# A list scheduler sets the order of gate, scan and q/k/v in a Hymba block; 22 of 32 exponent blocks skip DRAM

## The chip, the cores and the metric

The kernel runs on one core of a Trainium2 chip. The metric is the device time of one execution in microseconds. The core has a matrix engine (TensorE, PE in the profile), VectorE (DVE), ScalarE (ACT), GpSimd (POOL) and SyncE (SP), each with a queue of its own that it works through in order, and 16 DMA engines. In this kernel SyncE issues nearly all loads, ScalarE issues the stores of the stage spoken of here.

## The reference

One layer on x of 1024 tokens by 1024 features, all in float32. The layer has two mixers in parallel behind one input projection:

```
h = rmsnorm(x)
z, xbc, dt_raw, q, k, v = split(h @ w_in)          # 1024 | 1536 | 32 | 1024 | 1024 | 1024
y_ssm = ssd_mixer(z, xbc, dt_raw, ...)             # conv, bidirectional chunked scan, gate
y_na  = neighbourhood_attention(q, k, v, ...)      # q, k normalised by head, windows on a 16 x 64 grid
x = x + concat([y_ssm, y_na]) @ w_out
x = x + square(relu(rmsnorm(x) @ w_mlp_in)) @ w_mlp_out
```

The scan has 16 heads of 64 features in 2 groups, a state of 128 and chunks of 128 tokens. For each chunk, direction and head:

```
decay  = exp(where(lower, a_cum[l] - a_cum[s], -inf))       # 128 x 128 for a head
y_diag = (C B^T * decay) @ (x dt)                           # within the chunk
h      = chunk_decay * h + B^T (x dt * decay_to_end)        # state, chunk after chunk
y_off  = (C h) * exp(a_cum)                                 # carried into the chunk
y      = (y_f + y_b + d_skip x) * silu(z), then a grouped rmsnorm
```

## The kernel before

Every product of weight and activation is made as three products of halves: an operand is split into a rounded part and the rest (h and l in the names), and `mm3` multiplies high by high, high by low and low by high. The stages run one after another: the xBC projection with its convolution and the decays (0 to 172 us), then **gate, scan and q/k/v (172 to 648.5 us), the stage that is rewritten**, attention with w_out beside it (to 1034), and the two MLP products (to 1657).

The stage makes 64 pieces, each 128 tokens by 512 columns: 8 column blocks (z0 z1 q0 k0 v0 q1 k1 v1; 0 and 1 are the halves of the heads, with the scan's group of the same number) by 8 token blocks. A piece is 8 x 3 = 24 matmuls of 128x512 into one PSUM tile (`pz`, `pq`; L181 to L183 are the three of `mm3`). The weights of a column come as four tiles of 256 rows: a load `wraw` on SyncE (L150), the high half `wh` on ScalarE (L151), the low half `wl` on VectorE (L152). The rings of `wh` and `wl` hold four tiles, so a column's tiles take the place of the last one's; that of `wraw` holds three.

What follows a piece: for z a SiLU (L649) and a store. For q and k a square on ScalarE (`normed`, L330), a sum on VectorE (`sq`, L332), (mean + eps)^-0.5 on GpSimd (`rq`, L209 and L210), the scaling on VectorE (`qn`, L334), four transposes on TensorE (`ptq`, L342), the split into halves (`hl`, L194 and L195), and the store: four DMAs for q, one for k. For v the split and one store.

The scan's work lies between the pieces, written out by hand. `beside`, called behind each gate piece, makes the 14 states of the backward direction (`weighed` and its split, L416, L186, L187; `pS`, L617) and the first 20 exponent blocks. An exponent block holds four heads of a chunk, 128 x 512, for both directions: `seg_load` (L391) broadcasts the running sums of both directions to all partitions (`rb`, 512 KB), `seg_make` subtracts on GpSimd (two of L400) and selects by the mask of the lower triangle on VectorE (L406), `seg_store` (L411) puts the block into DRAM. All 32 blocks go that way, and `prepare` loads them again (`gm`, L688) and takes the exponential (L689). Behind the gate, the loop over 16 steps (2 groups by 8 chunks) takes pieces from the generator `qkv_units` between its parts: `carry` (the forward state), `inside` (C B^T, L705, and its product with the exponentials, L721), `carried` (L732, L733), `finish` (the inner product, `pd`, L758, and the gate, L675). The calls fix which piece stands between which parts; `issue_after` pins stores and some matmuls behind a piece. Within that, the framework orders each engine's queue.

Of the kernel before, what the change touches and what calls it, by code (L numbers as in the profile page):

```python
# [19 lines left out]
P = 128  # L20
# [9 lines left out]
HD = 64  # L30

# [25 lines left out]
def hymba_block(  # L57
# [35 lines left out]
    def enter_phase(ph, i, mm, extra):  # L93
        phase["ps"] = ph.enter_context(
            tc.tile_pool(name=f"ps{i}", bufs=1, space=PSUM, reuse_waits="tile")
        )
        phase["mm"] = mm
        phase["v"] = 4 - mm
        phase["w"] = [wp] * 3
        phase["r"] = [wp] * 2  # L100
        phase["n"] = 0
        if extra:
# [16 lines left out]
    q_dr = dr.tile([8, 4, HD, T], F32, name="q_dr")  # L119
# [4 lines left out]
    seg_dr = dr.tile([2, NT, P, 2, 512], F32, name="seg_dr")  # L124
    sb_dr = dr.tile([2, NT, P, 512], F32, name="sb_dr")
# [11 lines left out]
    def load_w(view, lo_eng, n=1024):  # L137
        pool = phase["w"][phase["n"] % len(phase["w"])]
        nb = phase["w"].count(pool)
        phase["n"] += 1  # L140
        rpool = phase["r"][phase["n"] % len(phase["r"])]
# [3 lines left out]
        hi = pool.tile([P, 1024], F32R, tag="wh", name="wh", bufs=nb)  # L145
        lo = pool.tile([P, 1024], F32R, tag="wl", name="wl", bufs=nb)
# [4 lines left out]
        nc.scalar.activation(hi[:, 0:n], raw[:, 0:n], AF.Copy)  # L151
        lo_eng.tensor_tensor(  # L152
            lo[:, 0:n], raw[:, 0:n], hi[:, 0:n].bitcast(F32), op=sub
        )
        return hi, lo

# [56 lines left out]
    with ExitStack() as ph:  # L213
# [98 lines left out]

        def hb(v):
            return v.unsqueeze(2).broadcast_to([P, 8, HD])

# [3 lines left out]
        def qkv_proj(off, g):  # L319
            get = load_w_nat(w_in[0], 0, KD, off + 512 * g, nc.vector)  # L320
            for b in range(NT):
                pt = ps_mm("pq")
                for k in range(KD):
                    s = (slice(None), k, slice(b * P, (b + 1) * P))
                    mark = mm3(pt, hTh[s], hTl[s], *get(k), k == 0, k == KD - 1)
                yield b, pt, rcol[:, b : b + 1], mark.ins

        def normed(pt, rt):
            qn = hp.tile([P, 512], F32, tag="qn", name="qn", bufs=2)
            act = nc.scalar.activation(qn, pt, AF.Square, scale=rt)  # L330
            ss = hp.tile([P, 8], F32, tag="sq", name="sq", bufs=2)
            nc.vector.tensor_reduce(ss, h8(qn), axis=mybir.AxisListType.X, op=add)  # L332
            r = inv_rms(hp, ss, HD, 8, "rq")
            nc.vector.scalar_tensor_tensor(h8(qn), h8(pt), rt, hb(r), op0=mul, op1=mul)  # L334
            return qn, act.ins

        def turned_split(qn, w, mark):
            tp = ps_tp("ptq")
            with tc.issue_after(mark):
                for j in range(4):  # L340
                    s = slice(j * P, (j + 1) * P)
                    nc.tensor.transpose(tp[:, s], qn[:, s], ident)  # L342
            hl = hp.tile([P, 2, 512], F32R, tag="hl", name="hl", bufs=2)
            split_from_psum(hl[:, 0], hl[:, 1], tp, w)
            return hl.bitcast(F32).rearrange("f a (p t) -> f a p t", p=4)

        def store_q(g, b, qn, mark):
            hl = turned_split(qn, pcol[:, 80:81], mark)
            s = slice(b * P, (b + 1) * P)
            for j in range(2):  # L350
                for a in range(2):
                    nc.scalar.dma_start(
                        q_dr[4 * g : 4 * g + 4, 2 * j + (a ^ j), :, s].rearrange("p d t -> d p t"),
                        hl[j * HD : (j + 1) * HD, a],
                    )

        def store_k(g, b, qn, mark):
            hl = turned_split(qn, pcol[:, 81:82], mark)
            nc.scalar.dma_start(
                k_dr[g, :, :, :, b * P : (b + 1) * P].rearrange("a p f t -> f (a p) t"),  # L360
                hl.rearrange("f a p t -> f (a p) t"),
            )

        def qkv_units():
            held = None
            for g in range(2):
                for off in (OFF_Q, OFF_K, OFF_V):
                    for b, pt, rt, mark in qkv_proj(off, g):
                        if held is not None:
                            held(mark)  # L370
                            held = None
                        if off == OFF_V:
                            hl = hp.tile([P, 8, 2, HD], F32R, tag="hl", name="hl", bufs=2)
                            split_from_psum(hl[:, :, 0], hl[:, :, 1], h8(pt), rt)
                            nc.scalar.dma_start(v_dr[b, :, 8 * g : 8 * g + 8], hl.bitcast(F32))
                            act = None
                        else:
                            qn, act = normed(pt, rt)
                            held = partial(store_q if off == OFF_Q else store_k, g, b, qn)
                        yield mark, act  # L380
# [7 lines left out]
        def seg_load(pool, bufs, g, c, q):  # L388
            rb = pool.tile([P, 2, 4, P], F32, tag="rb", name="rb", bufs=bufs)
            r0 = c * 16 + 8 * g + 4 * q  # L390
            nc.sync.dma_start(  # L391
                rb.rearrange("p d h s -> p d (h s)"),
                cum_dr[:, r0 : r0 + 4, :].rearrange("d h s -> d (h s)").partition_broadcast(P),
            )
            return rb

        def seg_make(rb, g, c, q):
            h0 = 8 * g + 4 * q
            for d in range(2):
                nc.gpsimd.tensor_tensor(  # L400
                    rb[:, d],
                    rb[:, d],
                    c1[:, d, c, h0 : h0 + 4].unsqueeze(2).broadcast_to([P, 4, P]),
                    op=sub,
                )
            nc.vector.copy_predicated(  # L406
                rb[:, 0], lmask.unsqueeze(1).broadcast_to([P, 4, P]), rb[:, 1]
            )
# [247 lines left out]
        with ExitStack() as p2:  # L656
# [140 lines left out]
            for _ in units:  # L797
                pass
# [676 lines left out]
```

## Time and profile before

| | |
|---|---|
| runs | 1654.14, 1653.69, 1646.92 us; median 1653.69 |
| profiled execution | 1659.05 us, span 1657.3 us |
| mean granted clock of TensorE | 0.982 |
| busy in the span | PE 1589.3 us (96%), DVE 1017.6 (61%), ACT 719.1 (43%), POOL 714.6 (43%) |
| stage 172 to 648.5 us | 476.5 us: PE 450.15 busy, DVE 293.28, ACT 173.80, POOL 274.82; clock 0.98, DMA 0.78 |
| DMA of the stage | 111.41 MB, 234 GB/s |

A busy PE is one on which a matmul is under way; two matmuls behind each other overlap in the record (0.39 us each, 0.227 apart). The arrow in a row names what ended an idle time. `pq`, `pz`, `ptq`, `pd`, `pS`, `py` are PSUM tiles by their use; `rb`, `gm`, `xhl`, `shl` SBUF tiles.

### The profile page before, as it was taken

Reading aid. Unit: us, or ns where it says so; the run is one execution under the profiler, and the core shown is the slowest. Engines: PE = TensorE matmul, PEld = TensorE weight load, DVE = VectorE, ACT = ScalarE, POOL = GpSimd, SP = SyncE. Lnnn points to the kernel's source line nnn. Section 1 sums busy time; section 2 is a strip of 40 time slices with the busy share of each in tenths; the row PEclk is TensorE's granted clock in tenths of the full one; section 3 lists DMA queues with packets and bytes.
Section 4 is the critical chain, followed back from the end, with each engine's and each line's share of the span. In section 5 each row is a group of like instructions: output and inputs, shape, how many; then the busy total and the mean of one; then the engine's idle time right before and its main releaser. Section 6 shows DMA issues by size and latency. Waiting matters only on the chain. (4 is left out here: it accounts for less than half of the span.)

```text
span 1657.3 us, 20925 instructions
## 1 busy us (share of the span) xinstructions
PE 1589.3 (96%) x7462; PEld 1300.0 (78%) x7462; DVE 1017.6 (61%) x1420; ACT 719.1 (43%) x1183; POOL 714.6 (43%) x520
## 2 busy tenths in 40 slices
PE   7999988998989999999998998999999989999999
PEld 6788867877867888887887776888888868888887
DVE  4777455477657773666665477434244388887863
ACT  5434322254334344566675334444444534433330
POOL 3000266467546744232353332344444555455551
PEclk9999999999999999999999998999999989999999
DMA  8113688897877669968772430453444486644332
GB/s 207 53 38 102 194 266 260 222 304 212 271 210 191 190 196 308 270 171 206 207 218 77 131 123 26 151 180 117 146 157 140 163 295 214 216 142 150 102 102 77
DMA packets 190243, 290.28 MB, mean 175 GB/s; under 512 B 15715, under 2 KB 106939, under 8 KB 190139
## 3 DMA queue, kind: packets, MB, share of 16 engines
q1 hardware_dynamic: 141547, 239.65, 47.4%
q10 hardware_dynamic: 47584, 45.62, 8.5%
q0 software_dynamic: 1008, 3.67, 0.5%
q8 instruction: 59, 0.97, 0.2%
q14 instruction: 45, 0.37, 0.1%
HBM read 197.27 MB, written 94.95 MB: 176 GB/s over the span
## 5 line engine op out<-in xcount | busy, mean ns | idle before, releaser
L187 POOL TENSOR_TENSOR wl<-wraw,wh 128x1024 fp32r<-128x1024 f32 x110 | 298.3, 2722 | 320.0 <-ACT wh L186 305.5
L186 ACT ACTIVATE wh<-wraw 128x1024 fp32r<-128x1024 f32 x110 | 115.5, 1054 | 150.1 <-PE px L804 50.7
L804 PE MATMUL px<-wh,ahl 128*128 128x512 f32 x512 | 162.4, 395 | 3.3 <-ACT ahl L186 3.3
L182 PE MATMUL pq<-wl,hTh 128*128 128x512 f32 x384 | 152.9, 399 | 6.7 <-DVE wl L152 6.7
L181 PE MATMUL pq<-wh,hTh 128*128 128x512 f32 x384 | 152.1, 401 | 7.0 <-ACT wh L151 5.3
L804 PE MATMUL px<-h,wh 128*128 128x512 f32 x496 | 156.0, 396 | 1.6 <-DVE x L1156 1.6
L183 PE MATMUL pq<-wh,hTl 128*128 128x512 f32 x384 | 152.4, 398 | 0.0
L187 DVE TENSOR_TENSOR ahl<-ar,ahl 128x1024 fp32r<-128x1024 f32 x56 | 114.7, 2055 | 23.3 <-ACT ahl L186 22.2
L186 ACT ACTIVATE ahl<-ar 128x1024 fp32r<-128x1024 f32 x56 | 58.2, 1052 | 140.0 <-PE px L804 76.4
L804 PEld LDWEIGHTS px<-wh,ahl 128*128 128x128 f32 x512 | 97.1, 190 | 25.0 <-ACT ahl L186 3.7
L804 PEld LDWEIGHTS px<-h,wh 128*128 128x128 f32 x496 | 93.2, 188 | 24.2 <-ACT h L191 1.8
L804 PE MATMUL px<-wl,ahl 128*128 128x512 f32 x256 | 100.9, 395 | 0.0
L400 POOL TENSOR_TENSOR rb<-rb,c 128x512 f32<-128x512 f32 x64 | 71.2, 1134 | 67.6 <-DMA rb<-cum_dr 57.0
L804 PE MATMUL px<-h,wl 128*128 128x512 f32 x248 | 98.1, 395 | 0.0
L182 PEld LDWEIGHTS pq<-wl,hTh 128*128 128x128 f32 x384 | 73.4, 191 | 22.9 <-DVE wl L152 8.4
L181 PEld LDWEIGHTS pq<-wh,hTh 128*128 128x128 f32 x384 | 73.2, 191 | 22.8 <-ACT wh L151 6.6
L151 ACT ACTIVATE wh<-wraw 128x1024 fp32r<-128x1024 f32 x58 | 60.6, 1057 | 66.8 <-DMA wraw<-in_w_in_dram 30.3
L191 ACT ACTIVATE pth<-ptp 128x384 fp32r<-128x384 f32 (+1 forms) x128 | 56.9, 457 | 66.0 <-PE ptp L1014 65.5
L183 PEld LDWEIGHTS pq<-wh,hTl 128*128 128x128 f32 x384 | 73.3, 191 | 15.0
L804 PE MATMUL pz<-h,wh 128*128 128x512 f32 x256 | 82.2, 402 | 0.4 <-DVE h L192 0.4
L804 PE MATMUL pz<-wh,ahl 128*128 128x512 f32 x256 | 80.5, 391 | 0.0
L181 PE MATMUL po<-wh,yh 128*128 128x512 f32 x192 | 76.5, 398 | 2.1 <-DVE x L888 1.8
(273 smaller groups left out, 4031.9 us busy)
## 6 DMA issues: line engine op xcount, KB each, us to landing
ar<-act_dr SPq DMA_DIRECT2D x56, 512.0 KB, 3.6
act_dr<-cq SPq DMA_DIRECT2D x49, 512.0 KB, 3.0
wraw<-in_w_in_dram SPq DMA_DIRECT2D x44, 512.0 KB, 4.3
rb<-cum_dr SPq DMA_DIRECT2D x32, 512.0 KB, 6.6
wraw<-in_w_mlp_in_dram SPq DMA_DIRECT2D x32, 512.0 KB, 4.7
wraw<-in_w_mlp_out_dram SPq DMA_DIRECT2D x32, 512.0 KB, 4.3
seg_dr<-rb ACTq DMA_DIRECT2D x32, 256.0 KB, 2.9
q_dr<-hl ACTq DMA_DIRECT2D x64, 128.0 KB, 3.8
```

The source lines that it names most:

```text
L151: nc.scalar.activation(hi[:, 0:n], raw[:, 0:n], AF.Copy)
L181: nc.tensor.matmul(pt, lhsT=ah, rhs=bh, start=first, stop=False)
L182: nc.tensor.matmul(pt, lhsT=ah, rhs=bl, start=False, stop=False)
L183: return nc.tensor.matmul(pt, lhsT=al, rhs=bh, start=False, stop=last)
L186: nc.scalar.activation(hl[0], src, AF.Copy)
L187: eng.tensor_tensor(hl[1], src, hl[0].bitcast(F32), op=sub)
L191: top = nc.scalar.activation(hi, src, AF.Copy)
L400: nc.gpsimd.tensor_tensor(rb[:, d], rb[:, d], c1[:, d, c, h0 : h0 + 4].unsqueeze(2).broadcast_to([P, 4, P]), op=sub,)
L804: nc.tensor.matmul(pt, lhsT=a, rhs=b, start=f, stop=l, skip_group_check=True)
```

## The change

`beside`, the loop over steps and the generator `qkv_units` are replaced by tasks: each instruction (or three or eight matmuls that belong together) is a `Task` with its engine, a length written by hand, the buffers it reads and writes, and for some a due time. `Plan.order` runs a list scheduler over them: it takes the task that can start first, in slots of 0.35 us, and among those the one due first. A task can start when its engine is free, what it depends on is over (plus a margin of 0.9 us for TensorE, 0.25 for the others) and the buffer that it takes in its ring is free; DMAs also queue for a modelled bandwidth. The kernel then emits the tasks in that order, and `in_order` ties every instruction to the one before it on its engine, so that the framework keeps the order. Besides:

- The columns come as z0 z1 q0 v0 k0 q1 v1 k1.
- 10 exponent blocks (the second four heads of steps 0 to 9) are still stored and loaded. The other 22 are made into the tile `seg` from which the step uses them. The subtraction for one direction writes `seg` or `y`, and the select (now L824) reads `rb`'s other half, so `rb` is free after the select; its ring holds 2.
- The ring of raw weights holds four tiles in place of three.
- q is laid out in DRAM like k and stored by one DMA of 512 KB a piece in place of four of 128 KB; attention loads it by four DMAs of 256 KB in place of one of 1024 KB.
- The DMAs that build the attention's bias table get due times through the stage; before they stood at its middle.

No product is added or removed on TensorE. The core of the diff:

```diff
+SCAN_TILES = (
+    ("rb", 2, 1024, F32),
+    ("seg", 4, 512, F32),
+    ("xs", 3, 512, F32),
+    ("xw", 1, 512, F32),
...
+class Plan:
+    MARGIN = {"PE": 0.9, "ACT": 0.25, "DVE": 0.25, "POOL": 0.25, "SP": 0.25}
...
+    def order(self):
+        for t in reversed(self.tasks):
+            if t.due is None:
+                t.due = 1e9
+            for u in t.after:
+                late = t.due - u.cost - self.latency(u)
+                u.due = late if u.due is None else min(u.due, late)
...
+            for t in todo:
+                at = self.ready(t, free)
+                if at is None:
+                    continue
+                key = (round(at / 0.35), t.due)
+                if best is None or key < best[0]:
+                    best = key, at, t
...
+    def ready(self, t, free):
+        e = "ACT" if t.eng == "AQ" else t.eng
+        at = free[e]
+        for u in t.after:
+            if u.end is None:
+                return None
+            far = u.eng != t.eng or u.size
+            at = max(at, u.end + (self.MARGIN[e] if far else 0.0))
+        for b in t.new:
+            if self.asked[b.tag][0] is not b:
+                return None
+            made = self.made[b.tag]
+            n = self.rings[b.tag]
+            if len(made) >= n:
+                for u in made[-n].users:
+                    if u.end is None:
+                        return None
+                    at = max(at, u.end + 0.2)
+        return at
...
-            phase["r"] += [wx]
+            phase["r"] += [wx] * 2
...
-    q_dr = dr.tile([8, 4, HD, T], F32, name="q_dr")
+    q_dr = dr.tile([2, 2, 4, P, T], F32, name="q_dr")
...
-        def seg_store(rb, g, c, q):
-            nc.scalar.dma_start(seg_dr[g, c, :, q], rb[:, 0].rearrange("p h s -> p (h s)"))
...
+        cols = [OFF_Z, OFF_Z + 512]
+        cols += [off + 512 * g for g in range(2) for off in (OFF_Q, OFF_V, OFF_K)]
...
+                task("SP", 0.45, load, writes=[raw], size=512, name="raw")
+                task("ACT", 1.06, high, reads=[raw], writes=[w], name="wh")
+                task("DVE", 1.7, partial(low, nc.vector), reads=[raw], writes=[w], name="wl")
...
+                task("POOL", 1.06, subtract, reads=[rb], writes=[rb] if d else [seg], name="sub")
+            task(
+                "DVE",
+                0.9,
+                lambda: nc.vector.copy_predicated(
+                    heads(seg.t), lmask.unsqueeze(1).broadcast_to([P, 4, P]), heads(both()[:, 1])
+                ),
+                reads=[rb],
+                writes=[seg],
+                due=due,
+                name="select",
+            )
...
+            task("PE", 0.95, within, reads=[*gm, xs], writes=[pd], due=at + 9, name="pd")
...
+        stored = [(n, 1) for n in range(10)]
...
+        for m, (c, g) in enumerate(back):
+            last[g] = back_state(c, g, last.get(g), when(6.0 + m))
+        for m, (n, q) in enumerate(stored):
+            exponents_stored(n, q, when(4.0 + 1.4 * m))
+        for n in range(16):
+            step(n, (0,) if (n, 1) in stored else (0, 1), when(20.0 + 2.4 * n))
+        tables()
...
+        for t in plan.order():
+            for buf in t.writes:
+                if buf.tag and buf.t is None and buf.tag not in ("w", "raw"):
+                    buf.t = tile_of(buf.tag)
+            with in_order():
+                t.emit()
```

What it does to the queues, at three places. The line numbers after the change are those of the new file. First VectorE, where it makes the low halves of q's first column (`wl`), of before:

```order
L187 TENSOR_TENSOR xhl<-xw,xhl 128x512
L406 COPY_PREDICATED rb<-lmask,rb 128x512
L617 TENSOR_TENSOR st<-st,pS 128x512
L406 COPY_PREDICATED rb<-lmask,rb 128x512
L187 TENSOR_TENSOR xhl<-xw,xhl 128x512
L152 TENSOR_TENSOR wl<-wraw,wh 128x1024 x3
L617 TENSOR_TENSOR st<-st,pS 128x512
L406 COPY_PREDICATED rb<-lmask,rb 128x512
L152 TENSOR_TENSOR wl<-wraw,wh 128x1024
```

and of the change:

```order
L824 COPY_PREDICATED y<-lmask,rb 128x512
L863 TENSOR_TENSOR yo<-yo,py 128x512
L846 TENSOR_TENSOR xl<-xw,xh 128x512
L712 TENSOR_TENSOR wl<-wraw,wh 128x1024 x4
L846 TENSOR_TENSOR xl<-xw,xh 128x512
L863 TENSOR_TENSOR yo<-yo,py 128x512
L824 COPY_PREDICATED seg<-lmask,rb 128x512
```

The select that stood between the third and the fourth low half now stands three instructions behind the four; one stands three ahead of them.

Second SyncE's queue, from the loads of the second gate column to those of q's first (both `wraw`), of before:

```order
L150 DMA wraw<-in_w_in_dram 128x2x512
L631 DMA xs<-xs_dr 128x512
L391 DMA rb<-cum_dr 128x2x512 x2
L631 DMA xs<-xs_dr 128x512
L391 DMA rb<-cum_dr 128x2x512 x7
L150 DMA wraw<-in_w_in_dram 128x2x512 x4
L391 DMA rb<-cum_dr 128x2x512 x3
```

and of the change:

```order
L975 DMA t_dr<-in_rel_pos_bias_dram 16x15x24 x8
L802 DMA rb<-cum_dr 128x2x512 x2
L851 DMA xs<-xs_dr 128x512 x2
L802 DMA rb<-cum_dr 128x2x512
L851 DMA xs<-xs_dr 128x512 x2
L284 DMA wraw<-in_w_in_dram 128x2x512 x3
L802 DMA rb<-cum_dr 128x2x512
L284 DMA wraw<-in_w_in_dram 128x2x512
L802 DMA rb<-cum_dr 128x2x512
```

Seven broadcasts (`rb`) stood in a run ahead of the four weight loads; now one or two stand between other loads, and three of the four weight loads come behind the third.

Third TensorE at the end of the stage, where the scores of attention (`psc`) and the turns of w_out's input (`pty`) begin, of before:

```order
L183 MATMUL pq<-wh,hTl 128x512
L985 MATMUL psc<-k,q 128x256
L988 MATMUL psc<-kl,q 128x256
L985 MATMUL psc<-k,q 128x384
L988 MATMUL psc<-kl,q 128x384
L862 MATMUL pty<-ident,yl 128x128 x8
```

and of the change:

```order
L326 MATMUL pq<-wh,hTl 128x512
L763 MATMUL ptq<-ident,qn 128x128 x4
L1213 MATMUL psc<-k,q 128x256
L1216 MATMUL psc<-kl,q 128x256
L1213 MATMUL psc<-k,q 128x384
L1216 MATMUL psc<-kl,q 128x384
L763 MATMUL ptq<-ident,qn 128x128 x8
L1085 MATMUL pty<-ident,yl 128x128 x4
```

The last column is now k, so the last product is followed by turns (`ptq`): four transposes of one piece at once, and eight of the last two behind the scores.

More of the change, by code (lines that the diff above doesn't have):

```diff
@@ L311, in hymba_block @@
         nc.sync.dma_start(dsk, d_skip.partition_broadcast(P)[:, 0, :])
-        def hb(v):
-            return v.unsqueeze(2).broadcast_to([P, 8, HD])
-        def h8(v):
-            return v.rearrange("p (e d) -> p e d", d=HD)
[L319 to L345, printed above, removed]
@@ new lines, in tile_of, with dma, when @@
+        def tile_of(tag):
+            if tag in make:
+                return make[tag]()
+            n, w, d = shape[tag]
+            return qs.tile([P, w], d, tag=tag, name=tag, bufs=n)
+        Buf, task = plan.buf, plan.task
+        def dma(eng, out, src, cost=0.45):
+            q = nc.sync if eng == "SP" else nc.scalar
+            return lambda: q.dma_start(out() if callable(out) else out, src() if callable(src) else src)
+        def when(k):
+            return 5.7 * k if k < 16 else 91.2 + 6.15 * (k - 16)
@@ new lines, in hymba_block, with w_view @@
+        cols = [OFF_Z, OFF_Z + 512]
+        cols += [off + 512 * g for g in range(2) for off in (OFF_Q, OFF_V, OFF_K)]
+        def w_view(j, k):
+            return w_in[0][256 * k : 256 * (k + 1), cols[j] : cols[j] + 512].rearrange(
+                "(a p) f -> p a f", p=P
+            )
+        first = [split_raw(r, nc.vector) for r in [load_raw(w_view(0, k)) for k in range(4)]]
+        W = {}
+        for k in range(4):
+            plan.given(Buf("raw"))
+            W[0, k] = plan.given(Buf("w"), first[k])
@@ L797, in hymba_block @@
-            for _ in units:
-                pass
+                task("SP", 0.45, partial(lambda i: nc.sync.dma_start(t2_dr[:, i], t1_dr[:, :, 15 - i : 31 - i, :].rearrange("h j r c -> h j (r c)")), i), reads=[*zero, *diag], size=250, due=260 + 6 * i, name="t2")
+        back = [(NT - 1 - m % 7, m // 7) for m in range(14)]
+        stored = [(n, 1) for n in range(10)]
+        last = {}
+        for j in range(8):
+            if j:
+                weights(j)
+            for b in range(NT):
+                piece(j, b)
@@ new lines, in hymba_block, with in_order @@
+        for m, (c, g) in enumerate(back):
[5 more added lines that the diff above has]
+        tables()
+        behind = {}
+        @contextmanager
+        def in_order():
+            traced = nc.cur_bb.bb.instructions
+            mark = traced[-1]
+            yield
+            start = next(i for i in reversed(range(len(traced))) if traced[i] is mark) + 1
+            for ins in traced[start:]:
+                if ins.engine in behind:
+                    tc.add_manual_dep(
+                        ins,
+                        behind[ins.engine].name,
+                        mybir.DependencyInfo(
+                            mybir.DependencyClass.NoSync, mybir.DependencyReason.DATA
+                        ),
+                        reason="issue_after",
+                    )
+                behind[ins.engine] = ins
```

621 lines of the change are left out of this document (356 added, 265 removed).

## The prediction

> **What bounds the kernel now.** I read the page's busy rows first, then the windows by stage, then the groups of TensorE with what ended their waits, and last the timeline and the waits of the other queues inside the stage that changes.
>
> ```profile
> PE 1589.3 (96%) x7462; PEld 1300.0 (78%) x7462; DVE 1017.6 (61%) x1420; ACT 719.1 (43%) x1183; POOL 714.6 (43%) x520
> 172.00:325.00 153.00, 143.69 (x621) 116.49 (x620) 76.81 (x78) 39.84 (x56) 85.64 (x78) 0.96 0.78 237
> 325.00:500.00 175.00, 159.56 (x775) 131.15 (x774) 120.17 (x188) 73.90 (x127) 106.53 (x101) 0.98 0.82 249
> 172.00:648.50 476.50, 450.15 (x2138) 371.05 (x2137) 293.28 (x417) 173.80 (x285) 274.82 (x261) 0.98 0.78 234
> ```
>
> A window row gives the stretch and its length, then PE, PEld, DVE, ACT and POOL (busy, instructions), the granted clock, the DMA share and GB/s. TensorE is busy 96% of the span, so no other engine bounds the whole. Only 172.0 to 648.5 us, gate, scan and q/k/v, is rewritten, so the gain can be no more than what TensorE loses there, in waits and in clock. Its groups in that stage say what that is:
>
> ```profile
> L182 PE MATMUL pq<-wl,hTh 128*128 128x512 f32 x384 | 152.9, 399 | 6.7 <-DVE wl L152 6.7
> L181 PE MATMUL pq<-wh,hTh 128*128 128x512 f32 x384 | 152.1, 401 | 7.0 <-ACT wh L151 5.3 <-DVE qn L334 1.7
> L182 PE MATMUL pz<-wl,hTh 128*128 128x512 f32 x128 | 51.2, 400 | 2.1 <-DVE wl L152 2.1
> L181 PE MATMUL pz<-wh,hTh 128*128 128x512 f32 x128 | 50.6, 399 | 2.3 <-ACT wh L151 2.3
> L342 PE MATMUL ptq<-ident,qn 128*128 128x128 f32 x128 | 19.8, 278 | 8.1 <-DVE qn L334 6.4 <-ACT gm L689 1.6
> ```
>
> Idle time is 6.7 + 7.0 + 2.1 + 2.3 + 8.1 = 26.2 us: 18.1 at the change from one weight column to the next, 8.1 at turns. The windows add the clock: 0.04 of 153 us is 6.1 and 0.02 of 175 us is 3.5, together 9.6. **The ceiling is 26.2 + 9.6 = 35.8 us.** One column change, TensorE first, then VectorE:
>
> ```profile
> 283.58 0.79 PE L182 MATMUL pq<-wl,hTh 128*128 128x512 f32 x1 [4.90 <-DVE wl L152]
> 284.18 0.63 PE L183 MATMUL pq<-wh,hTl 128*128 128x512 f32 x1
> ```
> ```profile
> 280.27 1.55 DVE L406 COPY_PREDICATED rb<-lmask,rb 128x512 f32<-128x512 int32 x1 [2.37 <-POOL rb L400]
> 281.72 0.67 DVE L187 TENSOR_TENSOR xhl<-xw,xhl 128x512 fp32r<-128x512 f32 x1
> 282.32 4.33 DVE L152 TENSOR_TENSOR wl<-wraw,wh 128x1024 fp32r<-128x1024 f32 x3
> ```
> ```profile
> ACT wh L151 <- DMA wraw<-in_w_in_dram: 29.9, 7, 10.5
> POOL rb L400 <- DMA rb<-cum_dr: 57.0, 20, 10.6
> DVE rb L406 <- POOL rb L400: 49.2, 24, 6.8
> ```
>
> The weights' low half stands in VectorE's queue behind a select that waits for a GpSimd subtraction, which waits for a broadcast transfer. TensorE idles 4.90 us, and the matmul after it takes 0.63 us instead of 0.40: half clock. The last fence totals such waits in the stage (sum, times, longest): late transfers, passed on by engines that keep their order.
>
> **The change, part by part.** *TensorE's work* is the same: 64 pieces of 24 products, the scan's products and the turns. Nothing there can give time but the 35.8 us.
>
> *Order.* The planner issues a column's four weight loads ahead of the broadcasts on SyncE, and VectorE makes all four low halves in one run (the order rows above). Each of the four links of the stall is thereby moved ahead of its use. I count the whole 35.8 us as removed, and add back what the new order brings.
>
> *Exponents.* 22 stores and 22 loads of 256 KB go, the 32 broadcasts of 512 KB stay. With 64 stores of q replaced by 16, ScalarE issues 70 transfers fewer (22 + 48). It was busy 173.80 of 476.50 us, so that lies beside TensorE: 0 us beyond the waits already counted. The bytes saved are 44 × 0.26 = 11.5 of 234 GB/s × 476.5 us = 111 MB; the DMA share stays near 0.78 × 0.9 × 476.5 / 458 = 0.73. Loads should land no later than before, and how late they were is in the 35.8: I take 0. If the saved bytes mattered for nothing but the waits on transfers, the worth is within that ceiling; if the share rose with the shorter stage, the loss is that of rival D.
>
> *Column changes that stay.* Even with raw weights in time, the four buffers of a column are reused by the next. Two rows of one change in the middle of the stage show the price where nothing was late:
>
> ```profile
> 353.06 0.96 PE L181 MATMUL pq<-wh,hTh 128*128 128x512 f32 x3 [0.41 <-ACT wh L151]
> 354.89 0.50 PE L182 MATMUL pq<-wl,hTh 128*128 128x512 f32 x1 [0.39 <-DVE wl L152]
> ```
>
> 0.41 + 0.39 = 0.8 us, seven changes: **+5.6 us**. If it were nothing 0, if all were like the late one above 7 × 4.9 = 34.
>
> *The dense stretch.* The new column order q, v, k puts k of the first half and q of the second back to back (from the start of piece 33 to that of 48, 15 pieces), and their normalising falls on VectorE together with the scan. By the order VectorE gets 8 low halves, 11 selects, 15 reductions, 15 scalings, 14 q/k low halves, 17 splits of scan operands, 13 decay products, 11 scalings of a carried part, 6 gate products and some 33 small or single ones. Their rows in the stage of before:
>
> ```profile
> L152 DVE TENSOR_TENSOR wl<-wraw,wh 128x1024 fp32r<-128x1024 f32 x29 | 38.5, 1347 | 0.8 <-ACT wh L151 0.8
> L406 DVE COPY_PREDICATED rb<-lmask,rb 128x512 f32<-128x512 int32 x32 | 39.6, 1239 | 54.2 <-POOL rb L400 49.2 <-DMA sz_dr<-zs 3.7 <-DMA wraw<-in_w_in_dram 1.3
> L332 DVE TENSOR_REDUCE sq<-qn 128x8 f32<-128x512 f32 x32 | 21.6, 677 | 4.7 <-ACT qn L330 4.6
> L334 DVE SCALAR_TENSOR_TENSOR qn<-pq,rcol,rq 128x512 f32<-128x512 f32 x32 | 24.0, 749 | 28.0 <-POOL rq L210 28.0
> L187 DVE TENSOR_TENSOR xhl<-xw,xhl 128x512 fp32r<-128x512 f32 x28 | 25.2, 900 | 21.7 <-ACT xhl L186 21.5
> 581.00:597.00 16.00, 16.00 (x86) 13.56 (x85) 14.62 (x22) 9.98 (x16) 12.29 (x11) 1.00 0.56 164
> ```
>
> Low halves, selects, reductions, scalings and splits come to 10.8 + 13.6 + 10.2 + 11.2 + 15.3 = 61.1 us, the other 77 at the mean of the second window (120.17 / 188 = 0.64) to 49: **some 110 us of VectorE**. TensorE's share of the same stretch, from three more prices:
>
> ```profile
> 1368.69 10.89 PE px L804 x48
> 303.22 0.60 PE L342 MATMUL ptq<-ident,qn 128*128 128x128 f32 x4
> 303.58 0.48 PE L181 MATMUL pq<-wh,hTh 128*128 128x512 f32 x1
> 579.27 1.90 PE L758 MATMUL pd<-xs,gm 128*128 128x64 f32 x16
> 580.97 0.48 PE L181 MATMUL pS<-xhl,bNh 128*128 128x512 f32 x1
> ```
>
> 10.89 / 48 = 0.227 a product, 0.36 a turn of four, 1.70 the inner product of a step. 15 pieces × 24 × 0.227 = 81.7, 45 scan products 10.2, 13 turns 4.7, 6 steps 10.2, some 1 for the rest: 108 us. VectorE would be the longer here. The last row of the fence before shows it filled to 14.62 of 16 us (91%) while TensorE never stopped; at that fill 110 / 0.91 = 121, a loss of 13. From below: a split can take 0.67 us (the row at 281.72) against its mean of 0.90; with 17 × 0.23, and 11 selects shorter in the same ratio (0.32 each), VectorE needs 7.4 us less, 103, which TensorE's 108 covers, and the loss is 0. I take **+7 us**, the middle: the row at 581 us speaks for the first end, the short splits for the second.
>
> The Trainium skill (page "SBUF — State Buffer", section "Who interferes with whom") says a VectorE instruction with two SBUF inputs contends with a GpSimd one that reads SBUF, and the later fully blocks. That speaks against so dense a stretch. The trace bears it out in part only: rival C below works out from rows what such an exclusion would cost here.
>
> *The end of the stage.* Before, v came last; now k of the second half does, whose last pieces must still be squared, reduced, normalised and turned. TensorE's queue holds the last two turns behind only four score products.
>
> ```profile
> 648.26 0.39 PE L183 MATMUL pq<-wh,hTl 128*128 128x512 f32 x1
> 648.49 0.28 PE L985 MATMUL psc<-k,q 128*128 128x256 f32 x1
> 649.07 1.04 PE L862 MATMUL pty<-ident,yl 128*128 128x128 f32 x8
> L209 POOL TENSOR_SCALAR rq<-sq 128x8 f32<-128x8 f32 x32 | 13.4, 420 | 29.4 <-DVE sq L332 27.8
> L210 POOL TENSOR_TENSOR rq<-rq,half 128x8 f32<-128x8 f32 x32 | 55.1, 1723 | 2.2
> L152 POOL TENSOR_TENSOR wl<-wraw,wh 128x1024 fp32r<-128x1024 f32 x2 | 4.7, 2393 | 10.3 <-ACT wh L151 10.3
> ```
>
> Before there is no gap at the border. After, the last piece's chain is a square on ScalarE (taken like the reduction, 0.68), then 0.68 + 0.42 + 1.72 + 0.75, together 4.25 us, less 0.94 of TensorE work in between (0.36 for a turn and 649.07 − 648.49 = 0.58 for the scores), and four hand-offs, an estimate of 0.4 each from the waits of 0.39 and 0.41 above: 4.25 − 0.94 + 1.6 = 4.9, **+5 us**. Two w_out splits of 2.39 us each stand on GpSimd just ahead of the last root; should they have to run after the reduction, it is 9.7.
>
> **Sum:** −35.8 + 5.6 + 7 + 5 = −18.2 us. The profiled execution took 1659.05 us (span 1657.3), 5.4 above the median 1653.69 of the three runs; I move the difference onto the median: **1635.5 us**, and 1641 for an execution like the profiled one.
>
> **Rivals.** *A, the plan holds nearly everywhere.* VectorE slides its work, columns change without a gap; only the end stays: −35.8 + 5 = −30.8, 1623. For it: the row at 581 us; against it: 110 us of VectorE in 108.
>
> *B, VectorE becomes the bound (slower).* Between pieces 17 and 57 the order puts some 243 us of VectorE (counted as above) beside 290 of TensorE. In before's densest window VectorE was filled 120.17 / 175 = 69%. If a fixed order on all five engines cannot fill it over 73%, the 40 pieces take 333 us, 43 more: −35.8 + 5.6 + 43 + 5 = +17.8, 1671.5. It decides below 77%, where the added 25 us eat the gain. For it: any late link now holds every engine, as the planner's lengths are not those of the trace (it counts a select at 0.9, the row says 1.24). Against it: 69% was also what was asked, not what was possible.
>
> *C, VectorE and GpSimd exclude each other on SBUF.* In pieces 33 to 48 GpSimd has 22 subtractions and some 29 other instructions of that size, 51 × 1.13 = 58 us, and 15 powers at 1.72, 26 us. VectorE's with two SBUF operands are the 15.3 + 13.6 + 10.8 = 40 us of splits, selects and low halves.
>
> ```profile
> L400 POOL TENSOR_TENSOR rb<-rb,c 128x512 f32<-128x512 f32 x64 | 71.2, 1134 | 67.6 <-DMA rb<-cum_dr 57.0 <-DVE yo L732 4.4 <-DMA sz_dr<-zs 4.3
> 363.95 1.65 POOL L210 TENSOR_TENSOR rq<-rq,half 128x8 f32<-128x8 f32 x1
> 365.23 0.68 DVE L187 TENSOR_TENSOR shl<-st,shl 128x512 fp32r<-128x512 f32 x1
> 280.20 1.04 POOL L616 TENSOR_TENSOR st<-st,ed 128x512 f32<-128x512 f32 x1
> ```
>
> A split beside a power is not stretched (0.68), the select at 280.27 beside a decay is (1.55). In series with all of GpSimd's work, 40 + 58 + 26 = 124 − 108 = 16 us of loss in place of 7: −9.2, 1644.5. In series with the 58 alone it is 98, and no loss, so the row at 365 us speaks against it.
>
> *D, the waits stay.* The transfers land as late as before (the share hardly falls) and the fixed orders pass it on: 0 gained, 5 lost at the end, 1659. Against it: the loads now stand several transfers further ahead on SyncE. That the order isn't kept is no rival: it stands in the order rows.
>
> **How the numbers follow.** Forecast 0.40 (own range 1627 to 1645), A 0.18, C 0.12, D 0.15, B 0.15. 0.5% is 8.3 us, about what a measurement of this kernel can tell from no change. Faster: forecast, A and half of C, 0.64; within: half of C and D, 0.21; slower: B, 0.15. The range takes in A with some 5 us below it, C, D and the lower half of B: 1617 to 1668.
>
> **What would show it.** Right: the stage lasts 455 to 460 us; the clock is 1.00 in it but for a short stretch at the end; waits of TensorE on the weights come to under 8 us, on turns to some 12, most of it in pieces 33 to 48 and at the last k, where a gap of 3 to 5 us stands before the double turn. B would show as VectorE above 90% with TensorE waiting for splits and scalings; D as waits for weights released by a DMA; C as splits over 1.4 us each time GpSimd works. Wrong altogether: a stage past 476.5 us, or a loss after 930 us, where nothing was changed.

## The result, and the profile after

The changed kernel takes 1638.78 us (median of 7 runs, 1637.26 to 1641.45) against 1656.41 for the kernel before, run beside it: a ratio of 0.9893, 95% interval 0.9863 to 0.9923. It is faster by some 17.7 us; 1635.5 had been predicted from the first three runs of before, a gain of 18.2. The profiled execution took 1640.9 us, its span 1639.1.

The page's busy row, the windows of the changed stage (whole; pieces 33 to 48; pieces 17 to 57) and of the border behind it, in the columns of the windows above:

```profile
PE 1581.6 (96%) x7462; PEld 1296.4 (79%) x7462; DVE 1021.6 (62%) x1420; ACT 721.3 (44%) x1183; POOL 715.6 (44%) x520
173.50:620.70 447.20, 439.83 (x2125) 366.12 (x2125) 291.81 (x413) 173.35 (x282) 273.82 (x258) 1.00 0.75 225
398.80:512.20 113.40, 112.44 (x582) 94.78 (x580) 89.78 (x138) 50.08 (x86) 86.78 (x85) 1.00 0.76 228
283.70:578.40 294.70, 292.76 (x1465) 245.40 (x1464) 227.60 (x346) 129.71 (x219) 202.75 (x196) 1.00 0.71 218
620.70:645.00 24.30, 16.68 (x85) 13.74 (x84) 11.69 (x22) 11.24 (x22) 13.59 (x13) 0.79 0.79 238
```

VectorE and GpSimd do the same work as before, within two microseconds (291.81 and 273.82 against 293.28 and 274.82), in a stage that is 29 us shorter. The clock is 1.00 over it as a whole; it falls short at the first column change (0.86 from 223 to 235 us) and in the border behind the stage (0.79). TensorE's groups between 173.5 and 645 us that waited for anything of weight:

```profile
L324 PE MATMUL pq<-wh,hTh 128*128 128x512 f32 x512 | 204.2, 399 | 1.0 <-ACT wh L709 0.6 <-ACT bh L917 0.3
L325 PE MATMUL pq<-wl,hTh 128*128 128x512 f32 x512 | 200.4, 391 | 1.8 <-DVE wl L712 1.8
L763 PE MATMUL ptq<-ident,qn 128*128 128x128 f32 x128 | 19.2, 272 | 4.1 <-DVE qn L759 4.1
L324 PE MATMUL py<-xh,bNh 128*128 128x512 f32 x28 | 12.1, 432 | 3.7 <-ACT xh L845 2.8 <-DVE yo L926 1.0
L324 PE MATMUL po<-wh,yh 128*128 128x512 f32 x8 | 4.2, 526 | 3.5 <-ACT yh L337 3.5
```

Of the 18.1 us at column changes 2.4 are left, all at one change; the 8.1 us at turns have become 4.1, all at the stage's end. New are 2.8 us for a backward state early in the gate and, behind the stage, 3.5 us at w_out's first product. Where the sum comes out can be read from four marks of the timeline, the first product of the stage, its last q/k/v product (648.26 before, quoted in the prediction), the last product of w_out's main part, and the last large product of the kernel. Of before:

```profile
172.01 0.39 PE L181 MATMUL pz<-wh,hTh 128*128 128x512 f32 x1
945.29 0.39 PE L183 MATMUL po<-wh,yl 128*128 128x512 f32 x1
1652.98 0.39 PE L804 MATMUL px<-wh,ahl 128*128 128x512 f32 x1
```

and of the change:

```profile
173.56 0.39 PE L324 MATMUL pq<-wh,hTh 128*128 128x512 f32 x1
620.47 0.39 PE L326 MATMUL pq<-wh,hTl 128*128 128x512 f32 x1
925.62 0.39 PE L326 MATMUL po<-wh,yl 128*128 128x512 f32 x1
1635.08 0.39 PE L1027 MATMUL px<-wh,ahl 128*128 128x512 f32 x1
```

So the stage takes 446.9 us in place of 476.3 (−29.3), from its end to the end of w_out's main part 305.2 in place of 297.0 (+8.1), the start is 1.6 later, and the rest takes 709.5 in place of 707.7. Together −17.9.

### The profile page after: what moved, and what is told of

The parts are those of the page before. It is cut to its first block, busy times and chain, and to the rows that moved or that the text cites. A ratio compares the mean times of both kernels' runs of the same rounds, so it can differ in the third digit from the quotient of the medians.

```text
span 1639.1 us, 20799 instructions
## 1 busy us (share of the span) xinstructions
PE 1581.6 (96%) x7462; PEld 1296.4 (79%) x7462; DVE 1021.6 (62%) x1420; ACT 721.3 (44%) x1183; POOL 715.6 (44%) x520
## 5 line engine op out<-in xcount | busy, mean ns | idle before, releaser
L330 POOL TENSOR_TENSOR wl<-wraw,wh 128x1024 fp32r<-128x1024 f32 x128 | 340.8, 2675 | 366.3 <-ACT wh L329 349.5
L329 ACT ACTIVATE wh<-wraw 128x1024 fp32r<-128x1024 f32 x140 | 147.2, 1056 | 181.4 <-PE px L1027 50.7
L324 PE MATMUL pq<-wh,hTh 128*128 128x512 f32 x512 | 204.2, 399 | 1.0 <-ACT wh L709 0.6
L325 PE MATMUL pq<-wl,hTh 128*128 128x512 f32 x512 | 200.4, 391 | 1.8 <-DVE wl L712 1.8
L326 PE MATMUL pq<-wh,hTl 128*128 128x512 f32 x512 | 200.7, 392 | 0.0
L325 PEld LDWEIGHTS pq<-wl,hTh 128*128 128x128 f32 x512 | 96.7, 189 | 21.4 <-DVE wl L712 2.1
L326 PEld LDWEIGHTS pq<-wh,hTl 128*128 128x128 f32 x512 | 96.4, 188 | 20.9
L324 PEld LDWEIGHTS pq<-wh,hTh 128*128 128x128 f32 x512 | 96.6, 189 | 20.6 <-ACT wh L709 1.1
L1164 POOL TENSOR_TENSOR mb<-braw,nam 128x256 f32<-128x256 f32 (+1 forms) x48 | 38.4, 829 | 92.9 <-DVE nmx L1221 70.3
L1231 ACT ACTIVATE pr<-pr,nmx 128x384 f32<-128x384 f32 (+1 forms) x128 | 74.9, 586 | 7.6 <-DVE nmx L1221 5.7
```

Source lines behind the costliest of these rows:

```text
L324: nc.tensor.matmul(pt, lhsT=ah, rhs=bh, start=first, stop=False)
L325: nc.tensor.matmul(pt, lhsT=ah, rhs=bl, start=False, stop=False)
L326: return nc.tensor.matmul(pt, lhsT=al, rhs=bh, start=False, stop=last)
L329: nc.scalar.activation(hl[0], src, AF.Copy)
L330: eng.tensor_tensor(hl[1], src, hl[0].bitcast(F32), op=sub)
L1164: nc.gpsimd.tensor_tensor(mb[:, s].rearrange("p (s r c) -> p s r c", r=16, c=8), v[:, a:b], nam[:, s].rearrange("p (s r c) -> p s r c", r= ...
```

## The experiments

The theory after the result: the order is the gain, that is, late selects no longer stand ahead of weights and turns; the bytes and transfers of the 22 blocks are worth nothing; the k column at the end takes back some 8 us. Rivals: bytes or transfers carry it; a simple late load did the harm; the border costs that much anyway. Ratios are to the kernel before, run on the same chip.

### v last

```diff
-        cols += [off + 512 * g for g in range(2) for off in (OFF_Q, OFF_V, OFF_K)]
+        cols += [OFF_Q, OFF_V, OFF_K, OFF_Q + 512, OFF_K + 512, OFF_V + 512]
...
-            return "z" if j < 2 else "qvk"[(j - 2) % 3]
+            return "z" if j < 2 else "qvkqkv"[j - 2]
```

> The changed kernel with one edit: in the second half the columns come as q, k, v in place of q, v, k, so that v is last, as before the change. Theory (the k column at the end costs some 8 us: waits of 4.12 and 3.50 us for the last turns and for the store that frees the split's buffer, and half clock behind them): the two waits go and the time falls from 1638.8 to 1630 to 1633 us, with the last product followed by scores within 1 us. Rival 1 (the border costs this anyway, since w_out's first turns wait for the same engines): 1637 to 1640. Rival 2 (three columns of q and k back to back, k0 q1 k1, fill VectorE past what TensorE covers): at least 1640, with TensorE waits on turns in the middle of the stage.

Measured: 1631.45 us, ratio 0.9862 (0.9820 to 0.9903). What happens at the border, of the change first, in the timelines of TensorE, GpSimd and ScalarE:

```profile
626.46 0.63 PE L763 MATMUL ptq<-ident,qn 128*128 128x128 f32 x4 [4.12 <-DVE qn L759]
631.52 0.79 PE L324 MATMUL po<-wh,yh 128*128 128x512 f32 x1 [3.50 <-ACT yh L337]
...
618.80 4.72 POOL L330 TENSOR_TENSOR wl<-wraw,wh 128x1024 fp32r<-128x1024 f32 x2
623.61 0.20 POOL L786 TENSOR_SCALAR rq<-sq 128x8 f32<-128x8 f32 x1
...
630.21 0.69 ACT L767 ACTIVATE hl<-ptq,pcol 128x512 fp32r<-128x512 f32 x1 [4.04 <-DMA k_dr<-hl]
630.79 0.68 ACT L337 ACTIVATE yh<-pty,pcol 128x512 fp32r<-128x512 f32 x1
```

and with v last:

```profile
625.42 0.39 PE L326 MATMUL pq<-wh,hTl 128*128 128x512 f32 x1
625.65 1.03 PE L1085 MATMUL pty<-ident,yl 128*128 128x128 f32 x8
626.45 0.47 PE L324 MATMUL po<-wh,yh 128*128 128x512 f32 x1
...
629.14 0.50 PE L325 MATMUL po<-wl,yh 128*128 128x512 f32 x1 [2.22 <-POOL wl L330]
```

Two gaps stand there in the change. The last turn waits 4.12 us for its chain, in which the root starts behind two splits of w_out on GpSimd. Then the first split of w_out's input waits on ScalarE behind the last split of k, which waits 4.04 us for an earlier store of k to free one of two buffers. With v last TensorE goes straight on into w_out, where it waits once, 2.22 us for a split of w_out's weights on GpSimd, and w_out's main part ends at 921.82, 296.4 us later: before's 297.0 again. Part of that is paid back in the stage, 452.1 us in place of 446.9 (four of the scores lie in it now, and TensorE waits 1.47 us for v's split among them). The theory holds at its place: k at the end cost the change 8 us there. Of the whole time some 5 us are gained (0.9862 against 0.9893), though the two intervals overlap; a later comparison, below, sets the change beside a kernel with v last.

### The table's loads later

```diff
-rel_pos_bias[0, :, :, 7 - j : 31 - j]), j), writes=[diag[j]]
+rel_pos_bias[0, :, :, 7 - j : 31 - j]), j), reads=[SB[0, 1]], writes=[diag[j]]
```

> The changed kernel with one edit: the eight strided loads of the bias table (9.26 us of SyncE's queue at 204 us in the profile) may start only when the last backward state is stored. Theory (these eight hold the broadcasts behind them, these the select, and the select the low halves of the second gate column): the waits of 0.65 and 1.80 us at 224 us and the 3.4 us of half clock behind them go, the wait of 2.76 us at 208 us may stay, as it comes from the ring of two tiles that the stored exponent blocks use; 1633 to 1636 us. Rival (the first broadcasts are late because the projections' stores end late, whatever stands behind them): 1638 to 1640.

Measured: 1635.10 us, ratio 0.9882 (0.9847 to 0.9917), not to be told from the change. The rows of the change that it was to mend, SyncE and TensorE:

```profile
203.84 9.26 SPq L975 DMA_DIRECT2D t_dr<-in_rel_pos_bias_dram  x8
213.19 1.05 SPq L802 DMA_DIRECT2D rb<-cum_dr  x2
...
211.61 0.50 PE L324 MATMUL py<-xh,bNh 128*128 128x512 f32 x1 [2.76 <-ACT xh L845]
224.66 0.50 PE L324 MATMUL pq<-wh,hTh 128*128 128x512 f32 x1 [0.65 <-ACT wh L709]
226.97 0.50 PE L325 MATMUL pq<-wl,hTh 128*128 128x512 f32 x1 [1.80 <-DVE wl L712]
```

The waits at 224 and 227 us are gone with the edit, as expected, and the clock from 223 to 237 us is 1.00. But the edit moves the whole plan behind it: a wait of 1.84 us stands at 216 us, and v's split is late at 531 and 543 us, 0.99 and 2.19 us. The mechanism at its place is shown; as a gain it is inconclusive.

### All 32 blocks stored, through the tile of y

```diff
-        stored = [(n, 1) for n in range(10)]
+        stored = [(n, q) for n in range(16) for q in range(2)]
...
-            step(n, (0,) if (n, 1) in stored else (0, 1), when(20.0 + 2.4 * n))
+            step(n, (), when(20.0 + 2.4 * n))
```

(and the blocks' due times closer together, 1.2 pieces in place of 1.4)

> The changed kernel with all 32 exponent blocks stored and loaded again (none used directly), still ordered by the planner. Theory (the gain comes from the order, not from the bytes): within 3 us of 1638.8, DMA share of the stage up from 0.75 to some 0.78, TensorE's waits in the stage still under 12 us. Rival (the 22 direct blocks carry the gain, by the 11.5 MB and the 44 transfers): 1645 to 1655, with waits on weights or turns that end with a DMA.

Measured: 1674.16 us, ratio 1.0123 (1.0088 to 1.0158). The theory's number is missed by some 35 us, and in its own profile TensorE waits all over the scan for VectorE. But the stored blocks and the steps' sums share two tiles of y, so the run mixes the store with a shortage of buffers. That called for the run in place, below.

### A fourth raw buffer in the kernel before

```diff
-            phase["r"] += [wx]
+            phase["r"] += [wx] * 2
...
+                if b == 2:
+                    raw_col(cols.index(off + 512 * g) + 1)
```

(`raw_col` issues the four loads of the next column; the same in the gate)

> The kernel before with one edit: a fourth buffer for raw weights, and a column's four loads written ahead by one column (behind its third piece). The order of VectorE's queue is that of before. Theory (much of the old waits came from the fourth weight tile, which a ring of three lets load only when the column changes; ScalarE's high half waited 10.5 and 9.3 us for it): the waits at 229 to 235 us, at 490 us and part of the others go, 1643 to 1650 us against 1656.4. Rival 1 (the list order does it, late tiles were not the point): 1653 to 1659. Rival 2 (the ring alone is all of it): 1636 to 1641.

Measured: 1661.38 us, ratio 1.0049 (1.0030 to 1.0067): slower. VectorE and TensorE at the first change to q, weights now in time:

```profile
281.24 1.55 DVE L443 COPY_PREDICATED rb<-lmask,rb 128x512 f32<-128x512 int32 x1 [3.40 <-POOL rb L437]
284.13 4.32 DVE L157 TENSOR_TENSOR wl<-wraw,wh 128x1024 fp32r<-128x1024 f32 x3
...
286.24 0.79 PE L190 MATMUL pq<-wl,hTh 128*128 128x512 f32 x1 [9.37 <-DVE wl L157]
```

The low halves stand behind the same late selects as before; TensorE waits 9.37 us in place of 4.90, and 8.67 at another change. The high halves on ScalarE no longer waited for a weight load (29.9 us before), so late weights were not the point: the theory of this run fell, and with it the prediction's reading of SyncE's queue. What the broadcasts themselves waited for stands in SyncE's queue, of before and then of this run:

```profile
SPq L391 <- DMA seg_dr<-rb: 94.2, 24, 8.6
```
```profile
SPq L428 <- DMA seg_dr<-rb: 99.1, 24, 10.0
```

It is the landing of an earlier block's store, which still reads the buffer.

### Two broadcast buffers in the kernel before

```diff
-                    made.append((seg_load(qp, 1, *sg), *sg))
+                    made.append((seg_load(qp, 2, *sg), *sg))
```

> The kernel before with one edit: two buffers in place of one for the broadcasts of the exponent blocks in the scan's half of the stage (the gate's half keeps its four). Theory now (the run with a fourth raw buffer showed it: VectorE stands at a select whose broadcast could start only when the block's store had left its buffer, and weights and turns stand behind the select): the waits from 325 us on shrink from some 20 us to under 10, 1642 to 1648 us against 1654. Rival 1 (the transfers are late for the DMA engines' load, not for the buffer): 1652 to 1656. Rival 2 (the order of the queues is what matters; a moved select hurts as often as it helps): 1650 to 1660 with other waits in place of the old ones.

Measured: 1647.72 us, ratio 0.9960 (0.9946 to 0.9973). Waits from 325 to 648.5 us on broadcasts, of before and with the edit:

```profile
POOL rb L400 <- DMA rb<-cum_dr: 33.2, 8, 10.6
DVE rb L406 <- POOL rb L400: 21.4, 6, 6.8
```
```profile
POOL rb L400 <- DMA rb<-cum_dr: 12.4, 8, 3.4
DVE rb L406 <- POOL rb L400: 6.0, 4, 3.6
```

TensorE's idle time falls from 17.0 us (325 to 648.5) to 10.2 (325 to 640, where the stage now ends). So in this half much of the lateness came from the buffer, which stayed taken until the block's store had read it. The gate's half, where nothing was edited, keeps its waits and has an 8.1 us one at the change to q.

### The bytes back, and the same with 2 KB

```diff
+            if tag == "seg":
+                put, src = Buf(None), xs_dr[c, :, g * 512 : (g + 1) * 512]
+                one, two = (dr.tile([P, 2, 512], F32, name=f"spare{n}{q}{i}") for i in "ab")
+                task("AQ", 0.42, lambda: nc.scalar.dma_start(one[:, q], src), reads=[done], writes=[put], size=256, due=due + 6, name="extra")
+                task("SP", 0.45, lambda: nc.sync.dma_start(two[:, q], one[:, q]), reads=[put], size=256, due=due + 12, name="extra")
```

(`done` is written by the select; the second kernel copies one row, `one[0:1, q]`, in each, and the planner is told the same size, so that its order is the same)

> The changed kernel with the 44 transfers of 256 KB put back as dummies: for each of the 22 direct blocks a copy from DRAM to DRAM issued by ScalarE once the select is over, and another issued by SyncE behind it. Nothing waits for them and no buffer of SBUF is held by them. Theory (the bytes and the issues are worth nothing by themselves): within 3 us of the changed kernel, 1634 to 1640, DMA share of the stage up by 0.05 to 0.08. Rival (bytes and queue time carry the gain of the direct blocks): 1645 or more, with waits on broadcasts and weights that end with a DMA.

> The kernel of the run with the bytes put back, with the same 44 dummy transfers in the same places of the same queues, each 2 KB in place of 256 KB; the rows of all five engines are otherwise the same. That run took some 23 us more than the change. Theory now (its bytes make the other transfers land later: v's store landed in 8.6 us in place of 4.5, and the split's ring of two waits for it): 1634 to 1641 us. Rival (the 22 waits that the dummies put into ScalarE's queue and the changed order do it): 1650 to 1660.

Measured: 1659.50 us, ratio 1.0027 (1.0013 to 1.0041), with the bytes; 1659.28 us, ratio 1.0025 (1.0013 to 1.0037), with 2 KB. The whole gain is lost both times, to the same tenth of a per cent, although the DMA share from 173 to 643 us is 0.79 in one and 0.70 in the other:

```profile
173.00:643.00 470.00, 452.20 (x2134) 373.42 (x2133) 297.63 (x413) 174.42 (x283) 273.72 (x258) 0.98 0.79 239
```
```profile
173.00:643.00 470.00, 451.31 (x2133) 372.05 (x2132) 295.90 (x413) 174.12 (x283) 273.11 (x258) 0.98 0.70 215
```

Nearly all the single waits are the same too. One of them, on TensorE and VectorE, with 256 KB and with 2 KB:

```profile
549.23 0.47 PE L324 MATMUL py<-sh,ch 128*128 128x512 f32 x1 [2.76 <-DVE yo L931]
546.97 1.55 DVE L824 COPY_PREDICATED seg<-lmask,rb 128x512 f32<-128x512 int32 x1 [0.94 <-POOL rb L813]
548.41 0.67 DVE L931 TENSOR_TENSOR yo<-py,e 128x512 f32<-128x512 f32 x1
```
```profile
552.09 0.47 PE L324 MATMUL py<-sh,ch 128*128 128x512 f32 x1 [2.78 <-DVE yo L931]
549.83 1.55 DVE L824 COPY_PREDICATED seg<-lmask,rb 128x512 f32<-128x512 int32 x1 [0.94 <-POOL rb L813]
551.27 0.67 DVE L931 TENSOR_TENSOR yo<-py,e 128x512 f32<-128x512 f32 x1
```

The scaling of a carried part stands behind a select that waits for GpSimd, and a matmul waits for the buffer that the scaling frees. The bytes are worth nothing in this order, which has lost its gain either way; the theory after the first of the two runs, that landing times had grown by the bytes, fell with the second. What the 44 dummies change is the queues: their own places, in ScalarE's behind a wait for the select, and the order that the planner makes around them. These two were not separated.

### All 32 stored in place

```diff
-            rb, seg = Buf("rb"), Buf(tag)
+            rb = Buf("rb")
+            seg = rb if tag == "rb" else Buf(tag)
...
-            seg = exponents(n, q, "y", due)
+            seg = exponents(n, q, "rb", due)
```

(with the edits of the first run with 32 stored; the subtractions and the select write into the broadcast's buffer)

> The changed kernel with all 32 exponent blocks stored and loaded as before the change, made in place in the broadcast's buffer (ring of two, held until the store has read it) in place of the tile of y; planned order. The run with 32 blocks stored through the two tiles of y took 37 us more than the change; the steps wait there for y. Theory (that run's loss came from the ring of y, and the order is the gain): 1636 to 1645. Rival 1 (stored blocks cost in any ring, since the store's landing holds a buffer that the next block or step needs): 1650 to 1675, with selects late on VectorE. Rival 2 (bytes): the same time as with the ring of y, 1670 to 1678.

Measured: 1657.31 us, ratio 1.0011 (0.9996 to 1.0027): 17 us better than through y, and still no gain over the kernel before. So the tile of y accounts for about half of that run's loss. Whether the other half comes from the buffer that is held until the store lands or only from a less lucky plan was not separated. Its longest wait, and what VectorE did ahead of it:

```profile
404.45 0.80 PE L324 MATMUL pq<-wh,hTh 128*128 128x512 f32 x1 [8.37 <-DVE hl L750]
400.24 1.55 DVE L825 COPY_PREDICATED rb<-lmask,rb 128x512 f32<-128x512 int32 x1 [1.93 <-POOL rb L814]
401.69 2.04 DVE L712 TENSOR_TENSOR wl<-wraw,wh 128x1024 fp32r<-128x1024 f32 x1
403.66 0.74 DVE L750 SCALAR_TENSOR_TENSOR hl<-pq,rcol,hl 128x512 fp32r<-128x512 f32 x1
```

A piece's PSUM tile is freed by VectorE's split of v, which stands behind a late select and a low half. A planned order by itself does not guarantee the gain.

### The order not held

```diff
-            with in_order():
-                t.emit()
+            t.emit()
```

> The changed kernel without the edges that hold each engine's queue in the planned order: the tasks are written out in that order, and the framework orders the queues as it did before the change. All buffers, the 22 direct blocks, the column order and the layout of q stay. Theory A (the order is the gain): 1648 to 1660. Theory B (the direct blocks and the buffers freed by the select are the gain, and the order adds little): 1634 to 1644.

Measured: 1659.42 us, ratio 1.0037 (1.0018 to 1.0055). Everything of the change is there but the held order, and nothing of the gain. TensorE waits up to 3.91 us for the backward states in the gate, 3.02 us for a step's sum in the scan, and 5.99 us at the border; the DMA share of its stage is 0.69, lower than the change's 0.75. The last of these waits:

```profile
652.00 1.08 PE L763 MATMUL ptq<-ident,qn 128*128 128x128 f32 x4 [5.99 <-DVE qn L759]
```

### Both edits, and then all blocks direct

The first kernel joins v last and the later table; the second also sets `stored = []`, so that all 32 blocks are made directly.

> The changed kernel with two edits together: the second half's columns as q, k, v, and the bias table's strided loads not before the last backward state. Theory (the two losses lie at different places and add): 1626 to 1631 us, the best so far. Rival (the tables' edit only shifts the late broadcasts elsewhere): as with v last alone, 1630 to 1633.

> The two edits together with all 32 exponent blocks made directly, none stored. Theory (each pair of a store and a load costs time by its bytes; 22 pairs put back cost some 23 us, so 10 fewer are worth up to 10): 1618 to 1628 us. Rival (the ten are made in the gate's columns, where the DMA engines and VectorE have room, and without them 10 more blocks fall into the scan, where VectorE and GpSimd are fullest): 1630 to 1645, with TensorE's waits on VectorE in the scan.

> The changed kernel itself, unedited, beside the three others on the same chip, so that they can be set against it: a ratio of 0.986 to 0.992 to the kernel before, as in the first comparison. If it lies outside, the runs of the three calls are compared by their ratios only within a call.

Measured beside each other: both edits 1632.15 us, ratio 0.9857 (0.9832 to 0.9882); all direct 1636.02 us, 0.9894 (0.9868 to 0.9920); the change again 1639.22 us, 0.9902 (0.9883 to 0.9922). Both edits beat the change by 7 us, the intervals just apart, and the kernel before by 1.4%. Against v last alone (0.9862) they cannot be told apart, so no gain of the second edit on top of the first is shown. The waits at 224 and 227 us and at the border are gone, one of 1.70 us stands at 216, and a new one near the end:

```profile
L324 PE MATMUL pq<-wh,hTh 128*128 128x512 f32 x512 | 205.2, 401 | 4.4 <-DVE hl L750 4.3
```

The ten blocks still stored are no visible loss: without them the time is, if anything, longer (the intervals overlap), and TensorE waits for VectorE at several places in the scan, the longest 2.49 us. That agrees with the rival, ten more blocks on the engines' fullest stretch, though the plan differs as well.

## Why the prediction was right, and where its steps were not

**The sum** of −18.2 met −17.7 because its errors cancel; that it came so close is luck. In the stage −23.2 had been forecast (−35.8 + 5.6 + 7) and −29.3 came; at the end +5, and +8.1 came. The rest, +1.6 at the start and +1.8 behind 925 us, was in no term. By the prediction's own signs the stage should have lasted 455 to 460 us; it lasted 446.9, so inside the stage rival A, by which the plan holds nearly everywhere, was nearer than the forecast.

**The ceiling** was read rightly: 35.8 us of waits and half clock, of which 29.3 went. No work left TensorE.

**Column changes:** +5.6 as seven times 0.8. One change cost anything, the first, 0.65 + 1.80 us of waits and some half clock behind them; the six others cost nothing that the groups show. The size is near, the reason was another: the eight table loads on SyncE ahead of the broadcasts, as the run with the later table shows.

**The dense stretch:** +7, and 113.40 − 112.44 = 1.0 us came. The step that failed is VectorE's 110 us: it was 89.78, for 138 instructions where the prediction had counted 143. The low halves and selects of this stretch:

```profile
L712 DVE TENSOR_TENSOR wl<-wraw,wh 128x1024 fp32r<-128x1024 f32 x8 | 9.7, 1221 | 1.6 <-ACT wh L709 1.4
L824 DVE COPY_PREDICATED seg<-lmask,rb 128x512 f32<-128x512 int32 x9 | 7.3, 836 | 0.3 <-POOL rb L813 0.3
```

A select took 0.84 there and not 1.24, a low half 1.22 and not 1.35. Low halves, selects, reductions, scalings and splits of 128x512 came to 53.3 us in place of 61.1, and the other 76 to 36.5 in place of 49, a mean of 0.48 and not 0.64. So the lower bound of 103 was itself too high, and 89.78 of 113.40 (79%) left TensorE alone.

**Rival C**, by which VectorE and GpSimd shut each other out, did not set the time in the dense stretch: those low halves, selects and splits, 9.7 + 7.3 + 15.7 = 32.7 us, and GpSimd's 86.78 come to 119.5, more than the 113.40 that passed, so some of them ran side by side. That weighs against the rule of the Trainium skill (page "SBUF — State Buffer", section "Who interferes with whom") as a price here; the trace shows its pattern at the first column change, where three low halves took 6.03 us beside GpSimd's work and not 4.33:

```profile
224.85 6.03 DVE L712 TENSOR_TENSOR wl<-wraw,wh 128x1024 fp32r<-128x1024 f32 x3
```

**The end:** +5, and 8.1 came. The first gap, 4.12, is the one described; GpSimd's two splits held the root back by some 0.8 us (the reduction ends at 622.75, the splits at 623.52). Missed was what is late next: ScalarE keeps its order too, so the first split of w_out's input waits behind a k split whose buffer a store still holds.

**Order and exponents:** here the reading was wrong although the sum was right. The prediction put the whole gain to the order and 0 to the 22 direct blocks, and let the weight loads stand behind the broadcasts as the first link. With a raw ring of three, the run of four loads in that queue is q's fourth tile and three of the next column; with all loads on time (the run with a fourth raw buffer) the waits grew. And the planned order with all blocks stored gave 1.0011, the direct blocks without the held order 1.0037. Neither half by itself gave anything, and without the held order the gain is gone. But a held order is not enough: the two kernels with dummies have both halves and stand at 1.0025 and 1.0027. Held plans of nearly the same work came out either at 0.986 to 0.990 (five of them) or at 1.001 to 1.012 (four), so a single plan without a part of the change says little about what that part is worth; for the direct blocks it stays open. That bytes are worth nothing was right as far as the two runs with dummies go.

**Rival B** did not come at 227.60 / 294.70 = 77% of VectorE over pieces 17 to 57, its own turning point: TensorE was busy 292.76 of 294.70. A fill of VectorE is no bound by itself. But its mechanism, one late link that holds every engine, is what the slower kernels look like: the same work, VectorE no fuller, and 20 us lost.

**Open:** why 44 small tasks more, or 22 more stored blocks, cost the planner's order so much. In the two kernels with dummies the same rows wait in the same places, and the planner's lengths (a select 0.9, a subtraction 1.06) are below what stands at the late places (1.55, up to 1.5); a plan with measured lengths was not tried. The single store of q for each piece and the fourth raw buffer were never taken out of the change by themselves.

## What to carry to other kernels

Where queues keep their order, look first at what stands ahead of the late instruction, not at what it reads: with the weights loaded earlier the kernel was 0.5% slower, their low halves still behind a select that waited for a broadcast. A buffer that only a store's landing frees is a wait on some engine later; free it by the compute that read it last. When an order is planned, test the pieces of the change one by one, since neither the order nor the shorter path need be worth anything alone, and try several plans: 44 tiny tasks more moved this kernel by 20 us. See also what the last column leaves for the next stage's engines.

## What the runs showed of the hardware that was not expected

The eight strided loads of the bias table (22.5 KB each) held SyncE's queue for 9.26 us. To issue one took 0.53 to 0.63 us, where a broadcast of 512 KB was issued in 0.37 (below); the other half of the 9.26 was waiting for earlier transfers to land. And 44 transfers of 256 KB more, 0.09 of DMA share over 470 us, moved the time by less than the measurement can tell from the same 44 with 2 KB: at a share of 0.70 or 0.79 alike, the bytes were not what set the time of this stage in that order.

```profile
222.54 0.37 SPq L802 DMA_DIRECT2D rb<-cum_dr  x1
```
